# A two-layer hybrid decoder trunk on one core: how one summed form, one exponential, the output's transposes and some low parts are made

## The chip, the cores and the metric

The kernel runs on one core of one Trainium2 chip. The metric is the device time of one execution in microseconds, the median of the runs shown; lower is better. The engines are named as the profile names them: PE (TensorE, matmuls and transposes), DVE (VectorE), ACT (ScalarE), POOL (GpSimd) and SP (SyncE, here a queue that only issues DMA). POOL issues DMA too.

## The reference

The input is x of 1 x 512 x 1024 in float32. Two layers follow, each a half-step SwiGLU, a mixer, and a half-step SwiGLU again. The mixer of layer 0 joins a Mamba-2 head group and an mLSTM head group; that of layer 1 is a sparse attention with an indexer and the top 256 keys of each query. Everything is float32.

```python
def rms_norm(x, g):
    y = xf * lax.rsqrt(jnp.mean(xf * xf, axis=-1, keepdims=True) + EPS) * g

def swiglu(h, w_gate, w_up, w_down):
    return (jax.nn.silu(h @ w_gate) * (h @ w_up)) @ w_down
...
x = x + 0.5 * swiglu(rms_norm(x, g), w_gate, w_up, w_down)
```

D is 1024 and the hidden width F is 2816. There are four of these feed-forward blocks; below they are ffn00 and ffn01 (layer 0, ahead of and behind its mixer) and ffn10 and ffn11 (layer 1). In layer 0 the Mamba-2 part needs A = -exp(a_log), a vector of 16 numbers.

## The kernel before

**Precision.** Each float32 operand of a product is held as two parts, a high one rounded to the type that PE takes and a low one, the rest. A product is three matmuls: high by high, high by low, low by high (lines 277 to 279). The two parts of a block together are called its form.

**How a form is made.** ACT writes the high part (line 416), and DVE subtracts it from the block to get the low part (line 418). For some blocks (`summed`) it goes another way: ACT writes the rounded block with its sign turned (line 451), a DMA that POOL issues adds the block to it (line 452), and ACT writes the high part (line 453); DVE has no part in it. Weight blocks come by SP's DMA into a ring of four raw buffers of 512 KB (384 KB in the last group), and the forms stand in a ring of five. A raw buffer is free when the last reader of it is done, the DMA of line 452 among them.

**A feed-forward block.** x is held transposed in `xT`. The 2816 hidden columns are 11 units of 256, in three groups: units 0 to 3, 4 to 7, 8 to 10. Units 0 and 1 (`unit`) are plain products of four weight blocks, g0 and g1 of the gate and u0 and u1 of the up matrix, into the banks `pg` and `pu`. The right side there is `xgn`, x times the norm's gain; the factor of each row is applied afterwards, so the products start before the norm is done. Between those products stand the sums of the squares: ACT squares a block (line 741), DVE adds it to `ssq` (line 411), PE sums over the partitions into `pssq` (line 382), DVE and POOL make the root (lines 695 and 697), PE turns it into rows (`prow`, line 391) and ACT copies these into `rrow` (line 701). The other units (`unit_seven`) and the down projection (`down`, twice seven products per group, one for each half of the output's columns) use a form of Strassen's algorithm with seven products of half size: left sides are the summed blocks A11, A12, S1, S2, S3, S4, A22. `keep` (ACT, line 574) copies a product that is used twice out of its bank.

**The summed blocks of the hidden units.** `forms` takes the hidden columns of a unit (tile `ft`), adds and subtracts blocks (DVE, line 411), and splits each of the results into parts (tiles `hid`, ACT line 416 and DVE line 418): A11 and A12 together, S1 and S2 together, S3 and A22 together, S4 alone. In the first half of the down projection, the products come in the order A11, A12, S1, S2, S4, S3, S4, A22.

**The end.** When the last group's half is done, DVE adds it into `xT` (line 788), PE turns 128 x 128 blocks back into the bank `pot` (line 816), ACT copies that into `ot` (line 825) and SP stores it (line 826). Four column pairs of 256 (`dp`) by two halves of the rows make eight stores.

**The order.** Nothing is issued when it is written down. A planner (`Plan`) collects all steps with costs and what they need, works out when each is due, and then takes step after step: the one that can start first, among these the one due first (its due time plus `later`). PE's steps stand in streams, each in its own order, and between the streams the same rule chooses. So an edit in one place can move steps of all engines elsewhere. Afterwards every engine runs its own list in order.

Of the kernel before, what the change touches and what calls it, by code (L numbers as in the profile page):

```python
# [12 lines left out]
AF = mybir.ActivationFunctionType  # L13
ALU = mybir.AluOpType
# [3 lines left out]
T = 512  # L18
# [206 lines left out]
class Trunk:  # L225
# [179 lines left out]
    def t(self, us, issue, reads, writes):  # L405
        self.plan.add("tensor", us, issue, reads, writes)
# [52 lines left out]
        self.count[tag] = n = self.count.get(tag, 0) + 1  # L459
        return Lazy(lambda: self.ps_two.tile([P, 2, T], F32, name=name, tag=tag)), (tag, n)  # L460

    def forms(self, t, tk):


        self.count["hid"] = n = self.count.get("hid", 0) + 1
        hi, lo = (Lazy(lambda: self.part.tile([P, 8, H], F32R, name="hid", tag="hid", bufs=8)) for _ in range(2))
        key = lambda part, a, b: [("hid", n, part, i) for i in range(a, b)]
        tt = lambda o, x, y, op: self.vtt(
            H, lambda: t()[:, o], lambda: t()[:, x], lambda: t()[:, y], op, [tk(o)], [tk(x), tk(y)]
        )  # L470

        def split(a, b, blocks):
            c = range(8)[blocks]
            self.parts(
                len(c) * H, lambda: hi()[:, a:b], lambda: lo()[:, a:b], lambda: t()[:, blocks], key(0, a, b), key(1, a, b),
                [tk(i) for i in c],
            )

        split(0, 2, slice(0, 4, 2))
        tt(4, 1, 3, ALU.add)  # L480
        tt(5, 4, 0, ALU.subtract)
        split(3, 5, slice(4, 6))
        tt(6, 0, 1, ALU.subtract)
        tt(7, 2, 5, ALU.subtract)
        split(5, 7, slice(6, 8))
        split(2, 3, slice(3, 4))
        return lambda i: (hi()[:, i], lo()[:, i]), lambda i: key(0, i, i + 1) + key(1, i, i + 1)
# [260 lines left out]
    def ffn(self, l, i, nxt, first=(), stream=iter(())):  # L748

        a = self.a  # L750
        wg, wu, wd = (a[n][l, i] for n in ("ffn_w_gate", "ffn_w_up", "ffn_w_down"))
        xf, tiles = [], [Lazy(lambda: self.part.tile([P, 2, 4, H], F32R, name="xf", tag="xf", bufs=7)) for _ in range(7)]
        self.count["xf"] = self.count.get("xf", 0) + 1
        for u0, u1 in GROUPS:
            hid = []
            for u in range(u0, u1):
                col = slice(u * 256, u * 256 + 256)
                raws = first if first and not u else [self.block(w[:, col], par) for w in (wg, wu) for par in range(2)]
                if u < EIGHT:
                    made = self.unit(raws, stream, bool(first) and not u, 3 * (1 - u) if first else 4)  # L760
                    next(made)
                    xf += self.xforms(2 * u, tiles)
                    t, tk = next(made)
                else:
                    t, tk = self.unit_seven(raws, xf)
                hid.append(self.forms(t, tk))
            self.down(wd[u0 * 256 : u1 * 256], hid, u1 == UNITS, nxt)

    def down(self, w, hid, final, nxt):
# [36 lines left out]
    def store_later(self, dp):  # L806

        nc = self.nc
        for b in range(0, NB, 2):
            pt = Lazy(lambda: self.aux("pot", (2, 256)))  # L810
            ot = Lazy(lambda: self.tmp.tile([P, 2, 256], F32, name="ot", tag="t1"))

            def turn(b=b, pt=pt):
                for bb in range(2):
                    for m in range(2):
                        nc.tensor.transpose(
                            pt()[:, bb, m * P : (m + 1) * P],
                            self.xT[:, 2 * dp + m, (b + bb) * P : (b + bb + 1) * P],
                            self.ident,
                        )  # L820

            rows = self.out[0, b * P : (b + 2) * P, dp * 256 : (dp + 1) * 256].rearrange("(b p) n -> p b n", p=P)
            pk, ok = [("pot", dp, b)], [("sq", b // 2)]
            self.t(0.5, turn, self.xk(2 * dp, (b // 2,)) + self.xk(2 * dp + 1, (b // 2,)), pk)
            self.s(T, lambda ot=ot, pt=pt: nc.scalar.activation(ot(), pt(), AF.Copy), pk, ok)
            self.plan.add("sync", 1.0, lambda ot=ot, rows=rows: nc.sync.dma_start(rows, ot()), ok, (), 2.0)

    def product_seven(self, raws, xf, kept, evac, tok, summed, scale):
# [141 lines left out]
    def hybrid(self, nxt):  # L970
# [7 lines left out]
        g = {}  # L978
        gates = self.gates(w, g)
        next(gates)  # L980
        tiles = [Lazy(lambda: self.part.tile([P, 2, 4, H], F32R, name="xf", tag="xf", bufs=7)) for _ in range(7)]
        self.count["xf"] = self.count.get("xf", 0) + 1
        chunks = lambda t, k: [(lambda i=i: t()[:, i], (*k, i)) for i in range(4)]
        bc = chunks(*self.spot("xs", (4, T), 1))
        u = self.unit_eight(self.columns(w, X0 + 1024), "hu", 3)
        next(gates)
        self.conv(u, 8, bc)
        xf = self.xforms(0, tiles)
# [78 lines left out]
    def hybrid_params(self):  # L1067

        nc, a, plan = self.nc, self.a, self.plan
        rows, rk = self.spot("hp", (P,), 1)  # L1070
        lo = 48

        def load(out, src, key):
            plan.add("sync", 0.6, lambda: nc.sync.dma_start(out(), src), (), key, 2.5)

        for r0, r1, name, form in (
            (48, 96, "hy_conv_w", "e k (c p) -> (e k c) p"), (96, 108, "hy_conv_b", "e (c p) -> (e c) p"),
            (108, 116, "hy_ssd_norm", "e (c p) -> (e c) p"), (116, 124, "hy_mlstm_norm", "e (c p) -> (e c) p"),
        ):
            load(lambda r0=r0, r1=r1: rows()[r0 - lo : r1 - lo], a[name].rearrange(form, p=P), [(*rk, r0)])  # L1080
        vec = self.consts[:, 7, 72:120]
        for o, n, name in ((0, 16, "hy_dt_bias"), (16, 4, "hy_fgate_bias"), (20, 4, "hy_igate_bias"), (24, 16, "hy_a_log")):
            load(lambda o=o, n=n: vec[:, o : o + n], a[name].partition_broadcast(P), [("vec", o)])
        ds = a["hy_d_skip"].rearrange("e (c two) -> two (e c)", two=2)
        for h in range(2):
            load(lambda h=h: vec[h * 64 : (h + 1) * 64, 40:48], ds[h].partition_broadcast(64), [("vec", 40, h)])
        self.gbias, self.nega, self.dskip = vec[:, 0:24], vec[:, 24:40], vec[:, 40:48]
        plan.stream = "ssd"
        pt, ptk = self.bank("hc")
        n = 124 - lo  # L1090
        self.t(0.2, lambda: nc.tensor.transpose(pt()[:, 0:n], rows()[0:n], self.ident[0:n, 0:n]), [(*rk, r) for r in (48, 96, 108, 116)], [ptk])
        self.v(n, lambda: nc.vector.tensor_copy(self.par[:, lo:124], pt()[:, 0:n]), [ptk], ["par2"])
        self.p(64, lambda: nc.gpsimd.affine_select(
            out=self.triu, in_=self.ones, pattern=[[1, P]], base=0, channel_multiplier=-1, compare_op=ALU.is_ge, fill=0.0
        ), (), ["triu"])
        self.p(64, lambda: nc.gpsimd.affine_select(
            out=self.last, in_=self.ones, pattern=[[0, P]], base=-(P - 1), channel_multiplier=1, compare_op=ALU.is_ge,
            fill=0.0,
        ), (), ["last"])
        self.s(16, lambda: nc.scalar.activation(self.nega, self.nega, AF.Exp), [("vec", 24)], [("vec", 24)], AF.Exp)  # L1100
        self.v(16, lambda: nc.vector.tensor_scalar(self.nega, self.nega, -1.0, None, op0=ALU.mult), [("vec", 24)], [("vec", 24)])

    def conv(self, u, c0, out):

# [61 lines left out]
    def gates(self, w, g):  # L1166


        nc, plan = self.nc, self.plan
# [10 lines left out]
                   [("f", j, 0), ("f", j, 1)] + xgk(k), [psk])  # L1180
        yield
        plan.stream = "ssd"
        t, tk = self.spot("gt", (T,), 1)
        self.v(T, lambda: nc.vector.tensor_tensor(t()[0:24], ps()[0:24], self.rrow[0:24], op=ALU.mult), [psk, "rrow"], [tk])
        pt, ptk = self.bank("hc")
# [10 lines left out]
        def st(n, kept=0):  # L1196
            used[kept] += NB * n
            box, at = boxes[kept], used[kept]
            return lambda: box()[:, at - NB * n : at].rearrange("p (b n) -> p b n", b=NB)
# [6 lines left out]
        x, u, s, z, p, vt = st(24), st(20), st(20), st(20), st(20, 1), st(20)  # L1206
# [833 lines left out]
```

## Time and profile before

| | |
|---|---|
| median of 3 runs | 1969.12 us (1965.04 to 1969.23) |
| the profiled execution's own time | 1967.11 us |
| its span | 1965.4 us |
| granted TensorE clock | 0.994 |
| busy: PE, DVE, ACT, POOL | 1926.9, 1637.0, 1262.0, 266.8 us |

All times of day in the trace are microseconds from the span's start. A row of the timeline gives the start, the length, the engine, the line, the operation and the tiles; in brackets stands how long the engine was idle ahead of it, and what ended that. Consecutive matmuls overlap by a pipeline, so a matmul of 0.39 us (512 columns) starts 0.23 us behind the one ahead of it, and one of 0.28 us (256 columns) 0.12 us behind.

### The profile page before, as it was taken

To read this page: it belongs to the slowest core of one execution; us is meant where nothing else is said; L and a number is where in the kernel's file an instruction comes from. 1 tells how busy PE (TensorE), PEld (TensorE's weight loads), DVE (VectorE), ACT (ScalarE), POOL (GpSimd) and SP (SyncE) were. 2 spreads that over 40 slices of the span, in tenths; PEclk is the share of its full clock that TensorE was granted. 3 is DMA by queue.
4 is the path that set the end of the run, shared out by engine and by line. 5 is a ranking of instruction groups with operands and counts; after the bars stand their busy time and mean duration, and the time that the engine had idled before them with its cause. 6 is when DMAs were issued, how large, how long until landed. Compare 5 with 4: busy or idle time off the path is not lost.

```text
span 1965.4 us, 36330 instructions
## 1 busy us (share of the span) xinstructions
PE 1926.9 (98%) x14631; PEld 1782.5 (91%) x14631; DVE 1637.0 (83%) x2425; ACT 1262.0 (64%) x1897; POOL 266.8 (14%) x360
## 2 busy tenths in 40 slices
PE   9999999999999999999999999999999999999998
PEld 7899999799898888999998899999856587999998
DVE  5998988999899559989898998888688747989886
ACT  6666767567667545667575566666757844757564
POOL 1000101112122100001010000010324410000000
PEclk9999999999999999999999999999999999999999
DMA  8566666467758343566664466765835202667664
GB/s 232 133 151 172 166 159 167 129 162 194 184 143 259 86 120 90 148 170 170 160 157 134 108 164 154 178 158 147 211 85 108 65 24 73 151 161 180 153 164 116
DMA packets 225600, 289.21 MB, mean 147 GB/s; under 512 B 14924, under 2 KB 196376, under 8 KB 224920
## 3 DMA queue, kind: packets, MB, share of 16 engines
q1 hardware_dynamic: 200728, 199.30, 32.9%
q0 software_dynamic: 24624, 87.57, 24.3%
q8 instruction: 115, 1.88, 0.4%
q14 instruction: 53, 0.43, 0.1%
q10 hardware_dynamic: 80, 0.02, 0.0%
HBM read 192.96 MB, written 6.33 MB: 101 GB/s over the span
## 4 chain that ended last, share of the span: by engine, by line
PE 84%; DVE 5%; DMA 4%; issue 3%; ACT 2%; POOL 1%; SPq 0%; ACTq 0%; POOLq 0%; DVEq 0%
PE pA L277 10%; PE pA L279 10%; PE pA L278 10%; PE pD L278 5%; PE pD L279 5%; PE pD L277 5%; PE hm L277 4%; PE hm L279 4%; PE hm L278 4%; PE pB L277 2%; PE pB L279 2%; PE pB L278 2%; DMA form<-raw 2%; PE pu L277 1%; PE pu L279 1%
## 5 line engine op out<-in xcount | busy, mean ns | idle before, releaser
L416 ACT ACTIVATE form<-raw 128x1024 fp32r<-128x1024 f32 (+2 forms) x389 | 399.0, 1030 | 202.0 <-DVE raw L411 109.7
L418 DVE TENSOR_TENSOR form<-raw,form 128x1024 fp32r<-128x1024 f32 (+2 forms) x389 | 461.5, 1192 | 67.9 <-ACT form L416 66.6
L411 DVE TENSOR_TENSOR raw<-raw 128x1024 f32<-128x1024 f32 (+2 forms) x281 | 333.0, 1194 | 11.9 <-DMA raw<-in_ffn_w_up 4.4
L452 POOL DMA_DIRECT2D form<-raw x165 | 144.1, 874 | 1340.2 <-ACT form L451 1108.5
L277 PE MATMUL pA<-xf,form 128*128 128x256 f32 x1152 | 320.4, 278 | 3.1 <-ACT ft L574 3.1
L279 PE MATMUL pA<-xf,form 128*128 128x256 f32 x1152 | 320.1, 278 | 0.5 <-DVE form L418 0.5
L278 PE MATMUL pA<-xf,form 128*128 128x256 f32 x1152 | 319.6, 277 | 0.0
L451 ACT ACTIVATE form<-raw 128x1024 fp32r<-128x1024 f32 (+1 forms) x165 | 170.4, 1035 | 123.6 <-PE pD L279 41.0
L277 PEld LDWEIGHTS pA<-xf,form 128*128 128x128 f32 x1152 | 216.7, 188 | 4.4 <-ACT ft L574 4.1
L279 PEld LDWEIGHTS pA<-xf,form 128*128 128x128 f32 x1152 | 216.9, 188 | 1.1 <-DVE form L418 1.1
L278 PEld LDWEIGHTS pA<-xf,form 128*128 128x128 f32 x1152 | 216.7, 188 | 0.2
L278 PE MATMUL pA<-hid,form 128*128 128x256 f32 x704 | 196.5, 279 | 3.3 <-DVE hid L418 3.3
L277 PE MATMUL pA<-hid,form 128*128 128x256 f32 x704 | 196.4, 279 | 0.0
L279 PE MATMUL pA<-hid,form 128*128 128x256 f32 x704 | 195.8, 278 | 0.0
L453 ACT ACTIVATE form<-raw 128x1024 fp32r<-128x1024 f32 (+1 forms) x165 | 169.2, 1026 | 0.0
L277 PE MATMUL pD<-xf,form 128*128 128x256 f32 x576 | 159.6, 277 | 0.0
L279 PE MATMUL pD<-xf,form 128*128 128x256 f32 x576 | 159.6, 277 | 0.0
L278 PE MATMUL pD<-xf,form 128*128 128x256 f32 x576 | 159.6, 277 | 0.0
L411 DVE TENSOR_TENSOR ft<-ft 128x256 f32<-128x256 f32 (+2 forms) x296 | 154.0, 543 | 3.8 <-ACT ft L681 0.3
L278 PEld LDWEIGHTS pA<-hid,form 128*128 128x128 f32 x704 | 132.4, 188 | 4.7 <-DVE hid L418 4.6
L277 PEld LDWEIGHTS pA<-hid,form 128*128 128x128 f32 x704 | 132.3, 188 | 0.7 <-ACT ft L574 0.2
L279 PEld LDWEIGHTS pA<-hid,form 128*128 128x128 f32 x704 | 132.5, 188 | 0.0
(455 smaller groups left out, 5293.3 us busy)
## 6 DMA issues: line engine op xcount, KB each, us to landing
form<-raw POOLq DMA_DIRECT2D x149, 512.0 KB, 5.9
raw<-in_ffn_w_gate SPq DMA_DIRECT2D x88, 512.0 KB, 5.1
raw<-in_ffn_w_up SPq DMA_DIRECT2D x88, 512.0 KB, 3.9
raw<-in_ffn_w_down SPq DMA_DIRECT2D x64, 512.0 KB, 4.5
raw<-in_hy_w_in SPq DMA_DIRECT2D x44, 512.0 KB, 5.0
raw<-in_ffn_w_down SPq DMA_DIRECT2D x32, 384.0 KB, 3.2
raw<-in_hy_w_out SPq DMA_DIRECT2D x16, 512.0 KB, 3.8
form<-raw POOLq DMA_DIRECT2D x16, 384.0 KB, 4.3
```

Of the source, the lines that this page charges most:

```text
L277: mm(out, l[0], r[0], start=start, stop=False)
L278: mm(out, l[0], r[1], start=False, stop=False)
L279: mm(out, l[1], r[0], start=False, stop=stop)
L411: (self.p if pool else self.v)(n, lambda: e.tensor_tensor(out(), x(), y(), op=op), reads, writes)
L416: self.s(n, lambda: nc.scalar.activation(hi(), src(), AF.Copy), srck, hik)
L418: n, lambda: nc.vector.tensor_tensor(lo(), src(), hi().bitcast(F32), op=ALU.subtract), srck + hik, lok
L451: self.s(n, lambda: nc.scalar.activation(f()[:, 1], raw, AF.Copy, scale=-1.0), rawk, lok)
L452: self.plan.add("gpsimd", 0.85, lambda: nc.gpsimd.dma_start(f()[:, 1], raw, accum_op=ALU.add), rawk + lok, lok, 6.0)
L453: self.s(n, lambda: nc.scalar.activation(f()[:, 0], raw, AF.Copy), rawk, hik)
```

## The change

There are four edits.

1. `forms` gets an argument `last`, true for the last unit of each group (units 3, 7 and 10). There, S1 is split into parts as soon as it is added, and S2 by itself behind it, where S1 and S2 were split together.
2. The exponential of a_log (one ACT instruction on 16 numbers, with a load of ACT's function table) and the DVE multiplication by -1 are written down behind the norm's rows of mixer 0, and the exponential needs `rrow`.
3. PE's transposes of the output stand in a stream of their own ("store") and are taken 10 us early in the planner's ranking. One of the eight copies out of `pot` goes to DVE (new line 833).
4. In units 0 and 1 of ffn01, ffn10 and ffn11 the up blocks u0 and u1 are `summed` (2 in place of 4): twelve blocks lose their subtraction on DVE and get a second ACT instruction and a DMA of POOL.

```diff
--- before.py
+++ after.py
@@ -459,7 +459,7 @@
         self.count[tag] = n = self.count.get(tag, 0) + 1
         return Lazy(lambda: self.ps_two.tile([P, 2, T], F32, name=name, tag=tag)), (tag, n)
 
-    def forms(self, t, tk):
+    def forms(self, t, tk, last=False):
 
 
         self.count["hid"] = n = self.count.get("hid", 0) + 1
@@ -478,8 +478,13 @@
 
         split(0, 2, slice(0, 4, 2))
         tt(4, 1, 3, ALU.add)
+        if last:
+            split(3, 4, slice(4, 5))
         tt(5, 4, 0, ALU.subtract)
-        split(3, 5, slice(4, 6))
+        if last:
+            split(4, 5, slice(5, 6))
+        else:
+            split(3, 5, slice(4, 6))
         tt(6, 0, 1, ALU.subtract)
         tt(7, 2, 5, ALU.subtract)
         split(5, 7, slice(6, 8))
@@ -757,13 +762,13 @@
                 col = slice(u * 256, u * 256 + 256)
                 raws = first if first and not u else [self.block(w[:, col], par) for w in (wg, wu) for par in range(2)]
                 if u < EIGHT:
-                    made = self.unit(raws, stream, bool(first) and not u, 3 * (1 - u) if first else 4)
+                    made = self.unit(raws, stream, bool(first) and not u, 3 * (1 - u) if first else 2)
                     next(made)
                     xf += self.xforms(2 * u, tiles)
                     t, tk = next(made)
                 else:
                     t, tk = self.unit_seven(raws, xf)
-                hid.append(self.forms(t, tk))
+                hid.append(self.forms(t, tk, u == u1 - 1))
             self.down(wd[u0 * 256 : u1 * 256], hid, u1 == UNITS, nxt)
 
     def down(self, w, hid, final, nxt):
@@ -821,8 +826,13 @@
 
             rows = self.out[0, b * P : (b + 2) * P, dp * 256 : (dp + 1) * 256].rearrange("(b p) n -> p b n", p=P)
             pk, ok = [("pot", dp, b)], [("sq", b // 2)]
+            stream, self.plan.stream, self.plan.later = self.plan.stream, "store", -10.0
             self.t(0.5, turn, self.xk(2 * dp, (b // 2,)) + self.xk(2 * dp + 1, (b // 2,)), pk)
-            self.s(T, lambda ot=ot, pt=pt: nc.scalar.activation(ot(), pt(), AF.Copy), pk, ok)
+            self.plan.stream, self.plan.later = stream, 0.0
+            if dp == 3 and b == 0:
+                self.v(T, lambda ot=ot, pt=pt: nc.vector.tensor_copy(ot(), pt()), pk, ok)
+            else:
+                self.s(T, lambda ot=ot, pt=pt: nc.scalar.activation(ot(), pt(), AF.Copy), pk, ok)
             self.plan.add("sync", 1.0, lambda ot=ot, rows=rows: nc.sync.dma_start(rows, ot()), ok, (), 2.0)
 
     def product_seven(self, raws, xf, kept, evac, tok, summed, scale):
@@ -1097,8 +1107,6 @@
             out=self.last, in_=self.ones, pattern=[[0, P]], base=-(P - 1), channel_multiplier=1, compare_op=ALU.is_ge,
             fill=0.0,
         ), (), ["last"])
-        self.s(16, lambda: nc.scalar.activation(self.nega, self.nega, AF.Exp), [("vec", 24)], [("vec", 24)], AF.Exp)
-        self.v(16, lambda: nc.vector.tensor_scalar(self.nega, self.nega, -1.0, None, op0=ALU.mult), [("vec", 24)], [("vec", 24)])
 
     def conv(self, u, c0, out):
 
@@ -1180,6 +1188,8 @@
                    [("f", j, 0), ("f", j, 1)] + xgk(k), [psk])
         yield
         plan.stream = "ssd"
+        self.s(16, lambda: nc.scalar.activation(self.nega, self.nega, AF.Exp), [("vec", 24), "rrow"], [("vec", 24)], AF.Exp)
+        self.v(16, lambda: nc.vector.tensor_scalar(self.nega, self.nega, -1.0, None, op0=ALU.mult), [("vec", 24)], [("vec", 24)])
         t, tk = self.spot("gt", (T,), 1)
         self.v(T, lambda: nc.vector.tensor_tensor(t()[0:24], ps()[0:24], self.rrow[0:24], op=ALU.mult), [psk, "rrow"], [tk])
         pt, ptk = self.bank("hc")
```

Lines of the changed kernel stand higher: 741 is 746, 732 is 737, 788 is 793, 816 is 821, 695 is 700, 701 is 706. The order of the engines' lists moves so in three places.

On DVE, in the last group of the last block (ffn11), where the hidden columns of unit 10 are made into forms; `form` are down weights, `hid` the hidden parts. Before:

```order
L411 TENSOR_TENSOR ft<-ft 128x256 x4
L418 TENSOR_TENSOR form<-raw,form 128x768
L418 TENSOR_TENSOR hid<-ft,hid 128x512
L418 TENSOR_TENSOR form<-raw,form 128x768
L418 TENSOR_TENSOR hid<-ft,hid 128x512
L418 TENSOR_TENSOR hid<-ft,hid 128x256
L411 TENSOR_TENSOR ft<-pB,ft 128x512
```

In the change:

```order
L411 TENSOR_TENSOR ft<-ft 128x256 x4
L418 TENSOR_TENSOR hid<-ft,hid 128x256 x2
L418 TENSOR_TENSOR form<-raw,form 128x768
L418 TENSOR_TENSOR hid<-ft,hid 128x512
L418 TENSOR_TENSOR form<-raw,form 128x768
L418 TENSOR_TENSOR hid<-ft,hid 128x256
L411 TENSOR_TENSOR ft<-pB,ft 128x512
```

The first two splits of 256 columns are now S1 and S2, each by itself; S1 has moved ahead of a subtraction of 768 columns, which stood between the additions and the split of both. The other three blocks' last groups read alike.

On DVE, at the start of ffn10, the last rows up to the mean of the squares (line 695, now 700); `raw` is `xT` on line 788 and a weight block on line 418, `xgn` the right side of the gate's and the up matrix's products. Before:

```order
L732 SCALAR_TENSOR_TENSOR xgn<-raw,xgn 128x512
L418 TENSOR_TENSOR form<-raw,form 128x1024
L411 TENSOR_TENSOR ssq<-ssq 128x512
L788 SCALAR_TENSOR_TENSOR raw<-ft,raw 128x2x256
L788 SCALAR_TENSOR_TENSOR raw<-pA,raw 128x2x256
L411 TENSOR_TENSOR ssq<-ssq 128x512
L418 TENSOR_TENSOR form<-raw,form 128x1024
L732 SCALAR_TENSOR_TENSOR xgn<-raw,xgn 128x512
L411 TENSOR_TENSOR ssq<-ssq 128x512 x2
L732 SCALAR_TENSOR_TENSOR xgn<-raw,xgn 128x512 x2
L695 TENSOR_SCALAR raw<-pssq 128x4
```

In the change:

```order
L737 SCALAR_TENSOR_TENSOR xgn<-raw,xgn 128x512
L793 SCALAR_TENSOR_TENSOR raw<-ft,raw 128x2x256
L793 SCALAR_TENSOR_TENSOR raw<-pA,raw 128x2x256
L411 TENSOR_TENSOR ssq<-ssq 128x512 x2
L737 SCALAR_TENSOR_TENSOR xgn<-raw,xgn 128x512
L418 TENSOR_TENSOR form<-raw,form 128x1024
L411 TENSOR_TENSOR ssq<-ssq 128x512 x2
L737 SCALAR_TENSOR_TENSOR xgn<-raw,xgn 128x512 x2
L700 TENSOR_SCALAR raw<-pssq 128x4
```

Of the two subtractions of 1024 columns (line 418) in these rows one is left. The additions into `xT` (line 788) follow each other, and the additions to `ssq` are the same in number.

On PE, in the tail, where the first four stores are turned. Before:

```order
L279 MATMUL pA<-hid,form 128x256
L277 MATMUL pA<-hid,form 128x256
L278 MATMUL pA<-hid,form 128x256
L279 MATMUL pA<-hid,form 128x256
L816 MATMUL pot<-raw 128x128 x16
L277 MATMUL pA<-hid,form 128x256
L278 MATMUL pA<-hid,form 128x256
L279 MATMUL pA<-hid,form 128x256
```

In the change, the first four of those sixteen transposes, and the other twelve 66 rows later:

```order
L277 MATMUL pA<-hid,form 128x256
L278 MATMUL pA<-hid,form 128x256
L279 MATMUL pA<-hid,form 128x256
L821 MATMUL pot<-raw 128x128 x4
L277 MATMUL pA<-hid,form 128x256
L278 MATMUL pA<-hid,form 128x256
L279 MATMUL pA<-hid,form 128x256
L277 MATMUL pD<-hid,form 128x256
```

```order
L277 MATMUL pD<-hid,form 128x256
L278 MATMUL pD<-hid,form 128x256
L279 MATMUL pD<-hid,form 128x256
L821 MATMUL pot<-raw 128x128 x12
L277 MATMUL pA<-hid,form 128x256
L278 MATMUL pA<-hid,form 128x256
L279 MATMUL pA<-hid,form 128x256
```

Between the four and the twelve now stand the last three matmuls of S3, the second part of S4 and all of A22 of the first half of the columns, and A11 and S1 of the second half (3 + 9 + 18 + 18 + 18 matmuls).

## The prediction

> **What bounds the kernel now.** I began with the page's first part and the view of PE's waits, each group with its total, its count and the longest.
>
> ```profile
> PE 1926.9 (98%) x14631; PEld 1782.5 (91%) x14631; DVE 1637.0 (83%) x2425; ACT 1262.0 (64%) x1897; POOL 266.8 (14%) x360
> PE pssq L382 <- DVE ssq L411: 5.8, 3, 2.5
> PE pD L278 <- DVE hid L418: 4.1, 4, 1.0
> PE pA L278 <- DVE hid L418: 3.3, 7, 1.2
> PE pA L277 <- ACT ft L574: 3.1, 5, 0.9
> ...
> PE pot L816 <- DVE raw L788: 1.0, 1, 1.0
> ```
>
> PE is busy for 1926.9 of 1965.4 us, and the change takes no matmul away. So what there is to win is its 38.5 us of idle time, and matmuls that run slowly. The five groups of waits hold 17.3 us of it; the other waits lie in places that the change hardly touches. DVE, busy for 83%, ends three of the five, ACT one. I therefore looked at each wait that an edit can reach, in the timeline, and asked of each what stands ahead of the late instruction on its engine.
>
> **Edit 1, S1 alone.** The four waits of `pD` on `hid` are one in the last group of each of the four blocks. That of ffn11 reads:
>
> ```profile
> 1927.21 2.28 DVE L411 TENSOR_TENSOR ft<-ft 128x512 f32<-128x512 f32 x5
> 1929.40 0.95 DVE L418 TENSOR_TENSOR form<-raw,form 128x768 fp32r<-128x768 f32 x1
> 1930.27 0.68 DVE L418 TENSOR_TENSOR hid<-ft,hid 128x512 fp32r<-128x512 f32 x1
> ...
> 1929.62 0.36 PE L277 MATMUL pD<-hid,form 128*128 128x256 f32 x1
> 1931.01 0.39 PE L278 MATMUL pD<-hid,form 128*128 128x256 f32 x1 [1.03 <-DVE hid L418]
> ...
> L418 DVE TENSOR_TENSOR hid<-ft,hid 128x256 fp32r<-128x256 f32 x44 | 18.4, 419 | 0.0
> ```
>
> PE wants the low part of S1 at about 1929.74, one matmul's pitch behind 1929.62. It is written by the subtraction that ends at 1930.95, because a weight form of 0.95 us stands ahead of it and it does S2 as well. In the new order the split of S1 comes straight behind the additions, which end at 1929.49: 1929.49 + 0.42 = 1929.9. Of 1.03 us some 0.15 stays at most, and the clumsy restart (0.36 and 0.39 us where 0.28 is usual) goes too, so I take the whole wait: 4.1 + 0.1 = **4.2 us** for four blocks. Bounds: 3.0, if ACT's high part of S1 comes 0.3 late each time, and 4.8. The price is one more instruction on ACT and one on DVE in each of twelve groups (2 x 0.42 us on DVE for one of 0.68, and about as much on ACT); DVE's weight form slips by 0.84 us, and its product comes behind the 18 matmuls of S1 (2.1 us), which covers it. If that cover is missing at a block, 0.8 us is lost there.
>
> **Edit 2, the exponential.** ACT's timeline around mixer 0's norm:
>
> ```profile
> 350.22 1.28 ACT L1100 ACT_TABLE_LOAD   x1
> 351.51 0.21 ACT L1100 ACTIVATE raw<-raw 128x16 f32<-128x16 f32 x1
> 351.64 1.04 ACT L416 ACTIVATE form<-raw 128x1024 fp32r<-128x1024 f32 x1
> 353.12 0.63 ACT L741 ACTIVATE ssq<-raw 128x512 f32<-128x512 f32 x1 [0.44 <-DVE ssq L411]
> 359.99 0.60 ACT L701 ACTIVATE raw<-prow 128x512 f32<-128x512 f32 x1 [6.24 <-PE prow L391]
> 362.73 1.82 ACT L416 ACTIVATE xf<-ft 128x512 fp32r<-128x512 f32 x3 [2.14 <-DVE ft L510]
> ```
>
> The 1.5 us leave a place where the last square, at 353.12, waited for DVE and not for ACT. They arrive in the 2.14 us in which ACT waits for DVE's line 510. Both ends are covered, so this edit is worth **0**; between a gain of 0.6 (one `xgn` row of DVE now stands earlier) and a loss of 0.3, if the load delays the first `xf`.
>
> **Edit 3, the stores.** PE's and DVE's rows at the first transposes:
>
> ```profile
> 1942.52 0.66 PE L816 MATMUL pot<-raw 128*128 128x128 f32 x4 [0.97 <-DVE raw L788]
> ...
> 1941.77 0.69 DVE L788 SCALAR_TENSOR_TENSOR raw<-pA,raw 128x512 f32<-128x512 f32 x1
> ```
>
> The second set of four waits for the addition of the product just finished. In the new order A11 and S1 of the other half stand in between (36 matmuls at a pitch of 0.12, about 4 us), so the wait goes: **1.0 us**. Their forms must then be there 2.7 us earlier (0.97 of wait, 12 transposes at 0.11 and the rest from edit 1). DVE's weight subtractions have moved up likewise. Bounds: 0 and 1.3. At the very end the chain is unchanged, the last product, transposes, a copy, a store; the copy on DVE takes one of the last ACT copies out of a row of four that are already paced by PE, so 0.
>
> **Edit 4, the up blocks.** Its largest place is the norm at the start of ffn10. The rows are DVE's, PE's, and the work on `pu` in two stretches (duration, busy time and count of PE, PEld and DVE, the granted clock, DMA; the second stretch is ffn11's):
>
> ```profile
> 1049.12 0.69 DVE L411 TENSOR_TENSOR ft<-pB,ft 128x512 f32<-128x512 f32 x1 [1.18 <-PE pB L279]
> ...
> 1058.86 1.23 DVE L418 TENSOR_TENSOR form<-raw,form 128x1024 fp32r<-128x1024 f32 x1
> ...
> 1062.39 1.23 DVE L418 TENSOR_TENSOR form<-raw,form 128x1024 fp32r<-128x1024 f32 x1
> 1063.53 0.76 DVE L732 SCALAR_TENSOR_TENSOR xgn<-raw,xgn 128x512 fp32r<-128x512 f32 x1
> 1064.19 1.42 DVE L411 TENSOR_TENSOR ssq<-ssq 128x512 f32<-128x512 f32 x2
> ...
> 1063.46 0.40 PE L279 MATMUL pu<-xgn,form 128*128 128x512 f32 x1
> 1065.76 1.52 PE L382 MATMUL pssq<-raw,ssq 128*128 128x1 f32 x8 [1.91 <-DVE ssq L411]
> ...
> 1067.00:1073.00 6.00, 5.47 (x12) 3.85 (x12) 0.00 (x0) 0.50 0.29 87
> 1632.70:1636.20 3.50, 3.46 (x8) 2.83 (x9) 0.00 (x0) 0.51 0.00 0
> ```
>
> Two things are lost there: a wait of 1.91 us, and behind it 6 us at a granted clock of 0.50, in which PE needs 5.47 us for 12 matmuls. From 1049.12 to the last addition to `ssq` DVE has no idle time worth a row, so what is taken off its list ahead of that addition brings it forward. One weight form less is 1.14 us (from its start to the next one's), and one `xgn` row (0.66) now stands ahead of 1049.12, where DVE idled for 1.18: the last addition ends at about 1064.0 instead of 1065.6, PE is done at 1063.8, and a wait of 0.1 to 0.5 is left. I take 0.5: **1.4 us** won. If the clock stays up, `pssq` takes the 1.02 us that it takes at mixer 0 (row below) instead of 1.52, and the 12 `pu` matmuls run at a pitch of some 0.23 us, 2.8 in place of some 5.2 (5.47 less the overlap of the last): 0.5 + 2.4 = **2.9 us**. That the clock stays up is read from mixer 0, where a longer wait than the one I expect left `pssq` at its full speed:
>
> ```profile
> 355.63 1.02 PE L382 MATMUL pssq<-raw,ssq 128*128 128x1 f32 x8 [1.31 <-DVE ssq L411]
> ```
>
> Bounds of these two terms: 0, if ACT's squares become the last thing in DVE's place, and 4.8. At ffn11 the same picture stands with 2.54 us, but there the chain is a product of the mixer, its addition, a square and an addition, whose rows keep their order; I count 0.
>
> The price of the edit: twelve blocks cost ACT 1.05 us more each and POOL one issue of 0.87, and DVE saves 1.22 each.
>
> ```profile
> L418 DVE TENSOR_TENSOR form<-raw,form 128x1024 fp32r<-128x1024 f32 x348 | 422.9, 1222 | 54.8 <-ACT form L416 53.6
> L451 ACT ACTIVATE form<-raw 128x1024 fp32r<-128x1024 f32 x149 | 157.0, 1056 | 109.0 <-PE pD L279 41.0 <-PE hm L279 20.7 <-PE pA L279 20.1
> DMA to landing us min/median/max: 3.9/5.8/10.7
> 797.98 0.39 PE L277 MATMUL pA<-xf,form 128*128 128x256 f32 x1 [0.86 <-ACT ft L574]
> ```
>
> A low part comes 1.06 + 5.8 = 6.9 us behind its raw block instead of some 2.3, and the raw buffer is held as much longer: on SP's queue the loads of g1 and u0 change places in ffn10, and on POOL's queue two such DMAs now stand ahead of the norm's root (line 697) in ffn01 and ffn10. Following ACT's new order with the old durations, the four up forms of ffn10 land 1.5 to 3 us before PE asks for them, so cover is there but thin. On the other side, in ffn01 the copy of line 574 now stands ahead of the next unit's work that delayed it at 797; that wait of 0.86 I count half, **0.4 us**. The other waits of the two groups on `pA` above (5.5 us in eleven) lie where rows changed places by one instruction; each can go or grow, and I set a loss of **1.0 us** for them.
>
> **The sum:** 4.2 + 0 + 1.0 + 1.4 + 2.9 + 0.4 - 1.0 = 8.9 us. The profiled execution took 1967.1 (span 1965.4 and 1.7 around it), so it would take 1958.2. The runs' median lies 2.0 above that execution and their lowest 2.1 below it; I put the median of the changed kernel at 1959.
>
> **Rivals.**
> *ACT takes DVE's place at ffn10.* Its list there got two pairs of lines 451 and 453, some 4.2 us, less two high parts, among the squares. Against it: in the old trace ACT idled over 1 us twice while it waited for DVE's additions. Then 4.3 us stay: 1963.
>
> *The up forms land late, and the kernel gets slower.* One mechanism: the DMA of line 452 moves 512 KB beside SP's loads, takes 8.5 to 10.7 us in place of 5.8, and PE waits at a unit's first `pu`. It decides once the landing is more than 3 us over the median. At four of the six units with 3 us each, and one stretch at half clock (2.4 as above), it costs 14: 1973. For it speaks the maximum of 10.7; against it that DMAs of this kind now make PE wait for less than 2 us in all.
>
> *Nothing is won overall.* The twelve extra ACT instructions stand ahead of copies that PE waits for, as at 797; if eight of them pass on 1 us, 1967.
>
> *More is won.* The half clock at ffn11 goes as well. Its idle stretch, the wait and `pssq`, is 3.6 us, that at ffn10 was 3.4, and that at mixer 0, which did no harm, 2.3; a cut of a few tenths might do, and would be worth eight matmuls (the second stretch above) at 0.2, with part of the wait some 2.5 us: 1956.5.
>
> ```profile
> 1631.82 1.06 PE L382 MATMUL pssq<-raw,ssq 128*128 128x1 f32 x8 [2.54 <-DVE ssq L411]
> ```
>
> The Trainium skill, "TensorE: Matmul & The Clock Gate", Part 1, says that the clock is halved after an idle window of about 3.4 us, and that the window runs freely. The trace agrees with the length (3.4 and 3.6 us did it, 2.3 did not); that the window runs freely no row here shows, and by it a stretch between these could fall either way.
>
> **How the numbers follow.** The forecast has 0.46, ACT in DVE's place 0.22, nothing won 0.16, late forms 0.10, more won 0.06. The forecast's own range is 1955 to 1963; with the neighbours the range is 1953 to 1967, which leaves out the late forms and part of "nothing". 0.2% (3.9 us) is what a measurement here tells from no change. Faster than that come out nearly all of the forecast, most of the first rival and the last one: 0.70. Slower: most of the late forms: 0.09. The rest, 0.21, is the same.
>
> **What would show it.** In PE's waits the four of `pD` on `hid` should be gone, and that of `pot`. At the start of ffn10 the `pssq` wait should be below 1 us, and the stretch behind it show a clock of 1.00; if it stays near 1.9 with ACT's squares ahead of the last addition, the first rival holds. A group of `pu` on a DMA of `form` would show the second. The sum is wrong if waits of `pA` on line 574 or on `hid` grow by more than 1 us.

## The result, and the profile after

The changed kernel took 1958.33 us, the median of six runs (1953.12 to 1961.34), the kernel before 1968.98 (six runs, 1965.04 to 1969.85): a ratio of 0.9945, with a 95% interval of 0.993 to 0.9961. The forecast was 1959 within 1953 to 1967, and faster. Run again on two other occasions the same kernel came out at 0.9966 (0.9953 to 0.9979) and 0.9965 (0.9952 to 0.9977). Over its 25 runs, each taken against the mean of the kernel before on the same occasion, the mean is 0.9962 with a standard error of 0.0003: some 7.5 us. The first six runs were on the lucky side; the forecast of 8.9 lies between.

The profiled execution took 1954.92 us with a span of 1953.0. Its page's first row, and the waits of PE that answer to those shown of before:

```profile
PE 1922.9 (98%) x14631; PEld 1781.7 (91%) x14631; DVE 1624.6 (83%) x2426; ACT 1273.3 (65%) x1920; POOL 276.7 (14%) x372
PE pssq L382 <- DVE ssq L411: 4.5, 3, 2.5
PE pA L278 <- DVE hid L418: 2.2, 6, 0.5
...
PE pD L278 <- DVE hid L418: 1.2, 2, 0.6
...
PE pA L277 <- ACT ft L579: 1.1, 2, 0.8
```

The four waits of `pD` of 1.0 us are gone, and two new ones of 0.6 stand in their group. `pot` is gone from the list. The wait on line 574 (now 579) fell from 3.1 to 1.1. DVE lost 12.4 us of work and ACT gained 11.3.

**S1 in ffn11**, DVE and PE:

```profile
1917.12 2.28 DVE L411 TENSOR_TENSOR ft<-ft 128x512 f32<-128x512 f32 x5
1919.31 0.75 DVE L418 TENSOR_TENSOR hid<-ft,hid 128x256 fp32r<-128x256 f32 x2
...
1919.63 0.28 PE L277 MATMUL pD<-hid,form 128*128 128x256 f32 x1
1919.78 0.39 PE L278 MATMUL pD<-hid,form 128*128 128x256 f32 x1
```

S1's low part comes straight behind the additions, and the product starts it 0.15 us behind its neighbour where it was 1.39. S1's 18 matmuls are 1.2 us shorter here; in ffn00, ffn01 and ffn10 they are 1.1, 1.3 and 1.3 shorter, 4.9 in all.

**The tail**:

```profile
1925.90 0.60 PE L821 MATMUL pot<-raw 128*128 128x128 f32 x4
...
1934.16 1.48 PE L821 MATMUL pot<-raw 128*128 128x128 f32 x12
```

Neither set waits.

**The norm of ffn10**, DVE and PE:

```profile
1063.58 1.22 DVE L418 TENSOR_TENSOR form<-raw,form 128x1024 fp32r<-128x1024 f32 x1
1064.72 1.41 DVE L411 TENSOR_TENSOR ssq<-ssq 128x512 f32<-128x512 f32 x2
...
1065.01 0.39 PE L279 MATMUL pu<-xgn,form 128*128 128x512 f32 x1
1066.18 1.05 PE L382 MATMUL pssq<-raw,ssq 128*128 128x1 f32 x8 [0.79 <-DVE ssq L411]
1067.10 0.48 PE L277 MATMUL pu<-xgn,form 128*128 128x512 f32 x1
```

The wait is 0.79 us where it was 1.91, and PE runs at full speed behind it. So far all is as forecast. But two other norms did what the forecast had not counted on. At mixer 0 a shorter wait than before (1.22 us for 1.31) was followed by a fallen clock, and at ffn11 the same wait as before (2.53 for 2.54) by none. The rows are `pssq`, and the busy times by stretches (as in the prediction, the first with ACT and POOL ahead of the clock, the second for `pu` alone):

```profile
355.25 1.12 PE L382 MATMUL pssq<-raw,ssq 128*128 128x1 f32 x8 [1.22 <-DVE ssq L411]
...
355.00:361.00 6.00, 5.75 (x25) 4.81 (x25) 2.77 (x5) 0.00 (x0) 1.94 (x1) 0.72 0.16 40
...
1626.72 1.05 PE L382 MATMUL pssq<-raw,ssq 128*128 128x1 f32 x8 [2.53 <-DVE ssq L411]
...
1627.00:1632.00 5.00, 3.00 (x12) 2.18 (x12) 0.00 (x0) 1.00 0.00 0
```

So the theory that the length of a wait tells whether the clock falls was in doubt, and with it what edit 4 is worth.

### The profile page after: what moved, and what is told of

The parts are those of the page before. It is cut to its first block, busy times and chain, and to the rows that moved or that the text cites. A ratio compares the mean times of both kernels' runs of the same rounds, so it can differ in the third digit from the quotient of the medians.

```text
span 1953.0 us, 36388 instructions
## 1 busy us (share of the span) xinstructions
PE 1922.9 (98%) x14631; PEld 1781.7 (91%) x14631; DVE 1624.6 (83%) x2426; ACT 1273.3 (65%) x1920; POOL 276.7 (14%) x372
## 4 chain that ended last, share of the span: by engine, by line
PE 81%; DVE 6%; DMA 6%; issue 4%; ACT 2%; POOL 1%; SPq 0%; ACTq 0%; POOLq 0%; DVEq 0%
PE pA L278 9%; PE pA L279 9%; PE pA L277 9%; PE pD L278 5%; PE pD L279 5%; PE pD L277 5%; PE hm L277 4%; PE hm L279 4%; PE hm L278 4%; PE pB L277 2%; PE pB L278 2%; PE pB L279 2%; DMA form<-raw 2%; PE pg L278 1%; PE pg L279 1%
## 5 line engine op out<-in xcount | busy, mean ns | idle before, releaser
L416 ACT ACTIVATE form<-raw 128x1024 fp32r<-128x1024 f32 (+1 forms) x377 | 386.7, 1030 | 222.2 <-DVE raw L411 130.0
L418 DVE TENSOR_TENSOR form<-raw,form 128x1024 fp32r<-128x1024 f32 (+1 forms) x377 | 447.2, 1191 | 65.7 <-ACT form L416 64.2
L452 POOL DMA_DIRECT2D form<-raw x177 | 154.5, 874 | 1387.8 <-ACT form L451 1102.3
L451 ACT ACTIVATE form<-raw 128x1024 fp32r<-128x1024 f32 (+1 forms) x177 | 183.1, 1037 | 115.8 <-PE pD L279 40.7
L453 ACT ACTIVATE form<-raw 128x1024 fp32r<-128x1024 f32 (+1 forms) x177 | 181.7, 1028 | 0.0
```

Of the source, the lines that this page charges most:

```text
L416: self.s(n, lambda: nc.scalar.activation(hi(), src(), AF.Copy), srck, hik)
L418: n, lambda: nc.vector.tensor_tensor(lo(), src(), hi().bitcast(F32), op=ALU.subtract), srck + hik, lok
L451: self.s(n, lambda: nc.scalar.activation(f()[:, 1], raw, AF.Copy, scale=-1.0), rawk, lok)
L452: self.plan.add("gpsimd", 0.85, lambda: nc.gpsimd.dma_start(f()[:, 1], raw, accum_op=ALU.add), rawk + lok, lok, 6.0)
L453: self.s(n, lambda: nc.scalar.activation(f()[:, 0], raw, AF.Copy), rawk, hik)
```

## The experiments

**Each edit alone.** Four kernels, each the kernel before with one of the four edits, timed together.

Edit 1:

```diff
-                hid.append(self.forms(t, tk))
+                hid.append(self.forms(t, tk, u == u1 - 1))
...
+        if last:
+            split(3, 4, slice(4, 5))
```

> Edit 1 alone (S1's form of each group's last unit made by itself), all else as before. My theory: the four waits of pD on hid in the last groups (1.0 us each) go and nothing else of size does: -4.2 us, ratio 0.9978. Rival (the planner's new order is what pays, not the wait): the four waits go, but waits of 0.5 us and more appear at other hid forms, and the sum is between -2 and 0. On the clock: the gap of 1.9 us at the start of ffn10 stays; if length alone decides, its 12 pu matmuls run at a granted clock of 0.5 as before; if the phase of a free-running window decides, the clock can be 1.0 there, or fall at mixer 0's norm instead.

Measured: 0.9988 (0.9978 to 0.9998); the mean of 12 runs lies 2.1 us under that of 35 of the kernel before (plus or minus 1.6, twice the standard error). The four waits were gone from the list. But at mixer 0's norm the wait grew:

```profile
352.05 2.35 DVE L418 TENSOR_TENSOR form<-raw,form 128x1024 fp32r<-128x1024 f32 x2
354.32 1.41 DVE L411 TENSOR_TENSOR ssq<-ssq 128x512 f32<-128x512 f32 x2
...
355.78 1.05 PE L382 MATMUL pssq<-raw,ssq 128*128 128x1 f32 x8 [2.37 <-DVE ssq L411]
```

Two weight forms stand ahead of the last squares where one stood before; the planner's new order put the second there. That takes 1.06 us back, and the clock fell behind it. A little ahead of that norm, near 349, PE's wait for `xgn` (line 278) grew from 0.32 to 0.92 us as well, in every kernel with edit 1. Neither the theory (4.2 net) nor the rival's place (other hid forms) is right: the gain at the four places is there in full, and a norm that had not been named for this edit took a part of it.

Edit 2:

```diff
-        self.s(16, ... self.nega, self.nega, AF.Exp), [("vec", 24)], [("vec", 24)], AF.Exp)
...
+        self.s(16, ... self.nega, self.nega, AF.Exp), [("vec", 24), "rrow"], [("vec", 24)], AF.Exp)
```

> Edit 2 alone (the exponential of a_log behind the norm's rows). My theory: 0 us, ratio 0.999 to 1.001; the wait of pssq on DVE's ssq in mixer 0 stays at 1.3 us, within 0.2. Rival: the 1.5 us of ACT were on the way to the last square, and the wait falls to under 0.5 us.

Measured: 0.9994 (0.9981 to 1.0007), and a wait of 1.31 us at mixer 0, as before. Worth nothing by itself, as forecast.

Edit 3:

```diff
+            stream, self.plan.stream, self.plan.later = self.plan.stream, "store", -10.0
             self.t(0.5, turn, ...)
+            self.plan.stream, self.plan.later = stream, 0.0
+            if dp == 3 and b == 0:
+                self.v(T, lambda ot=ot, pt=pt: nc.vector.tensor_copy(ot(), pt()), pk, ok)
```

> Edit 3 alone (the output's transposes as a stream of their own, one copy on DVE). My theory: the wait of pot on raw (0.97 us) goes and the tail from 1931 on is 1.0 to 1.5 us shorter: -1.2 us, ratio 0.9994; the last 4 us (transposes, copies, store) keep their length. Rival: the copy on DVE or the earlier demand for the second half's forms costs as much, and the tail is not shorter.

Measured: 0.9985 (0.9972 to 0.9997), 2.2 us plus or minus 2.2. The wait of `pot` was gone. From the end of S1 in the last block's first half to the end of the profile it is 32.05 us where it was 32.99: 0.9 us shorter, a little less than the 1.0 to 1.5 that were expected. PE is done 1.2 us earlier, but behind PE's last transpose the end takes 4.99 us in place of 4.75: the first of the four last copies is DVE's now, and ACT's begin 1.07 us behind the transposes' start where they began 0.64 behind it. The same kernel showed something else. Its wait at ffn10 is 1.90 us, as before, and the clock did not fall (the second row is `pu` alone):

```profile
1072.72 1.02 PE L382 MATMUL pssq<-raw,ssq 128*128 128x1 f32 x8 [1.90 <-DVE ssq L411]
...
1074.00:1080.00 6.00, 2.61 (x12) 1.80 (x10) 0.00 (x0) 1.00 0.29 90
```

Edit 4:

```diff
-                    made = self.unit(raws, stream, bool(first) and not u, 3 * (1 - u) if first else 4)
+                    made = self.unit(raws, stream, bool(first) and not u, 3 * (1 - u) if first else 2)
```

> Edit 4 alone (u0 and u1 of units 0 and 1 made by a DMA in three blocks). My theory: the pssq wait at ffn10 falls from 1.9 to 0.8 us or less, the clock stays at 1.0 behind it, and the wait of pA on line 574 in ffn01 (0.9) goes: -4.5 to -6 us, ratio 0.9973. Rival (clock by phase): the wait falls, but the half clock can come all the same, at ffn10, at ffn11 or at mixer 0, 1.5 to 2.5 us each; then the profile's gain is -1 to -3. Rival (ACT): the extra ACT work makes new waits on line 574, over 1 us in sum.

Measured: 0.9999 (0.9986 to 1.0012), 0.4 us plus or minus 2.2. The wait at ffn10 fell to 0.88 us, the clock stayed up there, and line 574's waits fell to 1.1, all as forecast; yet the time is the same. One thing that took it back is in PE's waits:

```profile
PE pD L278 <- DVE hid L418: 6.3, 6, 1.1
PE pssq L382 <- DVE ssq L411: 4.7, 3, 2.5
```

Two new waits of 1.1 us of `pD` on `hid` stand beside the old four of 1.0: in the first groups of ffn01 and ffn10, where DVE does a weight form ahead of S1's split. With edit 1 they are 0.6 each, in every kernel that has both edits.

**Without one edit, and the same kernels again.** To see edits 2 and 4 in company, and what the clock does to one and the same kernel, four more were timed together: all but edit 4, all but edit 2, the changed kernel, and the kernel before.

The two edits that are undone, against the changed kernel:

```diff
-                    made = self.unit(raws, stream, bool(first) and not u, 3 * (1 - u) if first else 2)
+                    made = self.unit(raws, stream, bool(first) and not u, 3 * (1 - u) if first else 4)
...
-        self.s(16, ... self.nega, self.nega, AF.Exp), [("vec", 24), "rrow"], [("vec", 24)], AF.Exp)
+        self.s(16, ... self.nega, self.nega, AF.Exp), [("vec", 24)], [("vec", 24)], AF.Exp)
```

> Edits 1, 2 and 3 together, the up blocks as before. My theory, by the single runs: the wait at ffn10 stays at 1.7 to 1.9 us, the waits of pD on hid in the last groups are gone: 1962 to 1964 us, ratio 0.997. Rival (edit 4 alone measured no gain, so it has none): 1958 us, as with it.

> Edits 1, 3 and 4, the exponential where it was. My theory, from the run with edit 1 alone, where mixer 0's norm waited 2.4 us instead of 1.3: without edit 2 that longer wait comes, 1.1 us and a half clock behind it (1.6 us): 1960 to 1961 us. Rival (the exponential is worth nothing): 1958 us and a wait of 1.2 us.

> The changed kernel once more, for a second profile and more runs. My theory: 1958 us again, ratio 0.9945; the wait of pssq at ffn10 is 0.8 us. Clock by length: mixer 0 slow again behind its 1.2 us, ffn11 at full clock again behind its 2.5 us, as in the first profile of this kernel. Clock by phase (rival): the same waits, but the slow stretches lie otherwise: at ffn11, or nowhere.

> The kernel before once more, for a second profile. Clock by length: 12 slow matmuls at ffn10, 7 at ffn11, none at mixer 0, as in its first profile. Clock by phase (rival): the waits are the same (1.3, 1.9, 2.5 us) and the number of slow matmuls behind them is another at one of the three at least. The wait of pA on hid at 1829 (1.17 us), which went with every edit, is there again if it belongs to the old order, and not if it is chance.

Measured: without edit 4 0.9962 (0.995 to 0.9975), without edit 2 0.9958 (0.9944 to 0.9973), the changed kernel 0.9966 (0.9953 to 0.9979), the kernel before 1.0 (0.9986 to 1.0014). Neither of the two edits can be told from nothing by the time. In the traces they can. Without edit 2 mixer 0's norm waits 2.36 us, as the theory said (in all kernels with edits 1 and 2 it is 1.2). Without edit 4 the waits on line 579 and at ffn10 are back:

```profile
PE pssq L382 <- DVE ssq L411: 5.5, 3, 2.5
PE pA L277 <- ACT ft L579: 3.0, 5, 0.9
```

The two second profiles decided on the clock. The kernel before, run again, had its three waits at 1.32, 1.90 and 2.54 us, to 0.01 as before, and this time the clock fell behind all three; here mixer 0, where the prediction had read that it stays up (PE, then a stretch of all engines' work):

```profile
356.17 1.02 PE L382 MATMUL pssq<-raw,ssq 128*128 128x1 f32 x8 [1.32 <-DVE ssq L411]
...
357.00:361.00 4.00, 4.00 (x14) 3.22 (x14) 1.68 (x5) 0.00 (x0) 1.94 (x1) 0.67 0.21 59
```

The changed kernel, run again, had full clock at all three. So the length of the wait does not settle it. The wait at 1829 of 1.17 us, which the first profile of before had, was not there; in the other profiles, but for the two of the filled kernels below, it is between 0 and 0.7 us. It was chance, and no edit's gain.

**Keeping PE busy through the waits.** Matmuls of ones into unused columns of the `pssq` bank, which nobody reads, were put ahead of the sums, in the same step, so that the order of everything else is unchanged: 4, 6 and 9 of them at mixer 0, ffn10 and ffn11 in the kernel with edits 1 to 3, and 4, 2 and 9 in the one with all four (each stands as two in the trace). The changed kernel ran beside them, and one with edit 4 in ffn11 alone.

```diff
+        for _ in range(fill):
+            self.nc.tensor.matmul(ps[:, P : 2 * P], self.ones, self.ones, start=True, stop=True)
         for b in range(NB):
```

> Edits 1, 2 and 3, the up blocks as before, and matmuls of ones that nobody reads ahead of the pssq matmuls, 4 at mixer 0, 6 at ffn10, 9 at ffn11 (about 0.22 us each, so that they end inside the waits of 1.2, 1.7 and 2.5 us). The order of all else is the same. Theory (the clock falls when PE does too little in a window that runs freely): no slow matmul behind any of the three, and the mean of the runs 2 to 4 us under that of the same kernel without them (ratio to the kernel before 0.9962 then): 0.994 to 0.995. Rival (the half clock has another cause, such as DMA or power): slow matmuls remain at ffn10 or ffn11, ratio 0.996.

> The changed kernel with the same matmuls of ones, 4, 2 and 9 of them, for waits of 1.2, 0.8 and 2.5 us. With the run before it, this tells what edit 4 is worth once the clock's chance is taken out. Theory by the traces (edit 4 takes 1.0 us of wait at ffn10 and up to 2 us of waits on line 574, and gives back 1.2 us at two hid forms): 1 to 2 us faster than the run without the up blocks. Rival by the times (it costs as much as it wins): the same, or 1 to 2 us slower. No slow matmuls behind the three norms in either case.

> The changed kernel a third time, beside the two with the matmuls of ones, on their chip. By the runs so far 6 to 10 us faster than the kernel before, ratio 0.9945 to 0.9966; slow matmuls at any of mixer 0 and ffn11, none at ffn10, where the wait is 0.8 us.

> All four edits, but the up blocks by DMA in ffn11 alone. By the traces ffn11 is the block that got shorter with edit 4 (322 us against 325), while ffn01 and ffn10 (330 and 336) did not. Theory: the gain of edit 4 is ffn11's, and this kernel is 2 to 3 us faster than the one with no up blocks by DMA, ratio 0.995. Rival: the 3 us were the clock's chance at ffn11 (0 slow matmuls in both profiles of the changed kernel), ratio 0.996, and ffn11's length is 325 us when the clock falls there.

The waits are filled, and the clock stays up at all three norms of both kernels. Of the first of the two, ffn11 (PE) and the three stretches:

```profile
1630.45 2.17 PE L383 MATMUL pssq<-raw 128*128 128x128 f32 x18
1633.14 1.05 PE L387 MATMUL pssq<-raw,ssq 128*128 128x1 f32 x8 [0.53 <-DVE ssq L416]
...
353.00:360.00 7.00, 6.66 (x40) 5.65 (x39) 4.48 (x7) 0.80 (x2) 1.94 (x1) 1.00 0.11 24
1067.00:1075.00 8.00, 7.44 (x44) 6.15 (x43) 6.11 (x9) 1.86 (x4) 2.60 (x1) 1.00 0.34 98
1626.00:1637.00 11.00, 10.47 (x77) 9.68 (x76) 5.13 (x10) 3.73 (x6) 1.03 (x1) 1.00 0.26 81
```

In the changed kernel beside them, the same wait of 2.54 us, not filled, brought one of the five longest slow stretches (6.83 us):

```profile
1627.96 1.87 PE L382 MATMUL pssq<-raw,ssq 128*128 128x1 f32 x8 [2.54 <-DVE ssq L411]
...
1629.00:1634.00 5.00, 4.30 (x10) 3.50 (x11) 0.00 (x0) 0.50 0.00 0
```

All twelve profiles without these matmuls, by the wait ahead of `pssq`:

| wait | place | clock fell behind it |
|---|---|---|
| 0.8 to 0.9 us | ffn10 with edit 4 | 0 of 5 |
| 1.2 to 1.3 us | mixer 0 | 3 of 10 |
| 1.7 to 1.9 us | ffn10 without edit 4 | 6 of 7 |
| 2.4 to 2.5 us | mixer 0 twice, ffn11 | 11 of 14 |
| filled, 0.3 to 0.5 left | all three | 0 of 6 |

Of these 20 falls, 15 last 3.41 us and 5 last 6.83. They slow 6 to 12 matmuls of 512 columns by about 0.2 us each: 1.2 to 2.5 us. A longer wait makes a fall likelier, and the same wait of the same kernel brings it or doesn't.

What decides stands in the profiles' records of the clock. In all fourteen, every stretch at 0.50 (but for the one cut off by the program's end) is 3.41 or 6.83 us long, and within a profile all of them begin and end on one grid of 3.413 us, to 0.002 us. Where this grid lies differs from execution to execution. Cut along it, mixer 0's norm in the kernel before, first profile and then second, reads (PE's matmuls on `xgn` alone, which leaves `pssq` out; then the clock and DMA):

```profile
352.74:356.15 3.41, 1.58 (x7) 1.00 0.05 0
356.15:359.56 3.41, 3.00 (x12) 1.00 0.12 29
...
354.97:358.38 3.41, 1.33 (x6) 1.00 0.06 6
358.38:361.80 3.42, 3.02 (x8) 0.50 0.37 116
```

The wait is the same, but the window that holds most of it has 1.58 us of other work in one execution and 1.33 in the other, and only behind the second does the clock fall. So it is at the three norms of all fourteen profiles: of the windows at full clock that touch a wait or its `pssq`, the 20 with a fall behind them have PE at work outside `pssq` for 0 to 0.41 of their length, the 44 others for 0.46 and more. The wait's length makes a fall likelier; where the grid lies is the chance. Busy time is not all that counts, though: near 1520, in mixer 1, the clock also fell behind windows in which PE was busy for 0.70, with smaller matmuls. The Trainium skill, "TensorE: Matmul & The Clock Gate", Part 1, has a window of 3413 ns that runs freely, and the fall behind an idle one. The trace agrees with the length and with the free run; but the windows ahead of a fall were not all idle here, with other work than `pssq` for up to 0.41.

In the times, the filled kernels are 0.9965 (0.9951 to 0.9978) without edit 4 and 0.9948 (0.9931 to 0.9966) with all four. The first is not the 2 to 4 us faster that were expected, but the same as without the filling (0.9962); the second, at 1959.93 us the lowest median of this set, lies 2.6 us under the mean of the changed kernel beside it, plus or minus 3.2. That the clock's fall is avoided is shown; that the filling pays in the run's time is not. Part of what it should win may have gone near 1829, where both filled profiles have two waits of PE on `hid`, 1.7 and 1.5 us in sum. That falls as such cost time agrees with the runs: over 205 of them, each against the mean of its kernel on that occasion, 1 us more at half clock (worked out from the run's granted clock) goes with 0.39 us more of time, plus or minus 0.08, so a fall of 3.41 us with some 1.3.

Edit 4 in ffn11 alone: 0.996 (0.9945 to 0.9974), and ffn11's length 326.3 us with a fallen clock: as the rival said.

**Where edit 4's gain went.** The stretches from one norm's `pssq` to the next, in the profiles of kernels that have edit 1 and no filling, in us:

| stretch | edit 4 in it | not in it |
|---|---|---|
| ffn01, with the wait at ffn10 | 329.1, 332.9, 331.0, 329.7 | 332.1, 329.8, 330.3 |
| ffn10 | 336.4, 335.1, 337.2, 338.0 | 337.5, 335.4, 336.7 |
| mixer 1 | 224.1, 224.1, 224.1, 224.1, 224.0 | 225.7, 225.6 |
| ffn11 | 321.0, 322.5, 324.2, 325.7, 326.3 | 325.1 |

(The kernel with edit 4 in ffn11 alone counts as "not in it" in the first two rows; ffn11 is taken from kernels that have edit 3 too.) In ffn01 and ffn10, where the waits at the norm and on line 574 went, the means are 330.7 and 330.7, 336.7 and 336.5: no gain. (The filled kernels have 328.9 and 336.9 us with edit 4, 332.4 and 339.1 without it; with them the means are 330.3 and 331.2, 336.7 and 337.2. Single profiles scatter by 3 us.) Two waits of 0.6 on `hid` are part of what came instead, and now and then a wait for the DMA of a form in the second group of ffn01:

```profile
931.84 0.38 PE L279 MATMUL pD<-xf,form 128*128 128x256 f32 x1 [0.92 <-DMA form<-raw]
```

Another part is the clock at ffn10's other end. Over all fourteen profiles ffn10 takes 335.1 to 336.9 us where the clock is at half for 3.41 us in it, 336.7 to 339.1 where for 6.83, and 340.5 where for 10.24. Of the four profiles with edit 4 in the table, none has a fall at ffn10's start, but all have one near its end (1389 to 1398), 6.83 us long in two of them; of the three without, two have one of 3.41 us there and one has none. Nor is there less half clock over the whole of the runs: the mean granted clock is 0.9946 with edit 4 alone (12 runs) and 0.9955 for the kernel before beside it (35), 0.9956 with all four edits (25) and 0.9958 without edit 4 (11).

What else took the gain back, up to some 2 us over the two blocks, has no single place: it lies in stretches in which PE falls behind by 0.3 us over tens of microseconds without a wait. What causes that is open. Mixer 1 is shorter by 1.5 us in the left column, but that is not edit 4's gain either. With edit 4 alone it takes 225.7 us, and without edit 4, in the filled kernel, 224.0 (PE's busy time, the clock and DMA from norm to norm):

```profile
1405.88:1631.56 225.68, 219.95 (x1238) 0.99 0.39 92
...
1409.10:1633.14 224.04, 220.52 (x1256) 1.00 0.37 85
```

The seven profiles in which the clock falls near 1520 for 3.41 us have 225.5 to 226.0, the seven in which it does not have 224.0 to 224.1. What keeps it up there in some kernels is open. In ffn11 the two shortest of the left column, 321.0 and 322.5, are those without a fall at its norm; a gain of perhaps 1 us is left. The runs' times (0.4 plus or minus 2.2 alone; 0.1 plus or minus 1.7 for the 25 runs of the changed kernel against the 23 without edit 4, filled or not; 2.8 plus or minus 3.4 between the two filled kernels) allow a gain of 1 or 2 us and not 4.7.

## Why the prediction was right, and where it was not

The time, the sign and the size came out. The reasons did so in part.

- **Edit 1** (4.2): right in place and cause. The four places gave 4.9 in the traces. Alone it paid 2.1 plus or minus 1.6: the planner lengthened two waits at mixer 0 at the same time, by 1.06 and 0.6 us, and with edit 2 the first of these is gone.
- **Edit 2** (0): right alone. In company it is what keeps mixer 0's wait at 1.2 and not 2.4 us, a gain of 1.1 in the trace that I had not seen, since I read its worth only in the old order. In the times neither shows.
- **Edit 3** (1.0): right in its place; 0.9 in the trace, of which 1.2 at PE, less 0.25 at the very end, which I had put at 0; 2.2 plus or minus 2.2 in time.
- **Edit 4's wait** (1.4): the mechanism was right, the size 1.1. A last wait of 0.8 stayed, not 0.5.
- **Edit 4's clock** (2.9): this step failed. "That the clock stays up is read from mixer 0" took one profile's one stretch for a rule; in the kernel's second profile the clock fell there too. Whether it falls depends on how PE's work lies in windows of 3.41 us, whose place differs from execution to execution; the profile of before had drawn the costliest of seven at ffn10 (6.83 us and 12 slow matmuls; the others 8, 8, 7, 7, 6 and none). On the average, a wait of 1.7 to 1.9 us costs some 7 slow matmuls at 0.2, so 1.4 us and not 2.9 were to be had. The fall at ffn10 did go (none in five), but half clock over the whole run did not get less.
- **Line 574** (0.4): the sum of its waits fell by 2.0, in every kernel with edit 4 in all three blocks. Mis-sized; I had counted one of its places only.
- **The unforeseen** (a loss of 1.0): the two new waits on `hid` are 1.2 us with edit 1, 2.2 without. The size is right; that edit 4 loses the rest of its 4.7 us too was not foreseen.
- **ffn11** (0): the wait stayed at 2.53, as said. The first profile's gain there was the clock's chance.
- **The rivals**: late forms did not come; a wait of up to 0.9 us for the DMA of a form stands in the feed-forward blocks at times, but one of 0.7 does in the kernel before too. ACT did not take DVE's place at ffn10. Nearest to the truth comes "nothing is won", for edit 4 alone.

That the sum held is in part luck: edits 1 to 3, which I had put at 5.2, measured 7.8 plus or minus 1.9 (the mean of 11 runs against the kernel before), and edit 4, put at 4.7, about none. What gave the 2.6 us more than I had put is not shown.

## What to carry to other kernels

Before a slow stretch behind a wait is counted as a gain, look at the same place in a second profile of the same kernel: what changes there without an edit is a chance, and is worth its mean. In a program whose order a planner makes, an edit's worth depends on the others, because each moves work at places that it does not name; so look at every wait again after each. And a wait that goes is a gain of time only if the stretch around it gets shorter.

## What the hardware showed

At the three norms the granted clock fell to half behind a pause of PE of 1.2 us and up, at the same place of the same kernel in one execution and not in another, and did so in none of six cases where matmuls of ones filled the pause. Each fall lasted 3.41 or 6.83 us and lay on a grid of 3.413 us; the window ahead of it held other work than the one-column matmuls of `pssq` for at most 0.41 of its length, where 0.46 and more brought no fall. Two executions of one kernel differed by up to 9 us (span 1953.0 and 1961.9), with no edit between them: 3.3 us in mixer 0, where waits for the DMA of a form came and went (0.7 and 2.1 us at one place), 3.8 in ffn01 (the wait of 0.92 shown above is one of them), and the rest spread thin, much of it a slow drift without a wait.
